# One fixed order for rows, weight halves and products at the three norm boundaries of a two-layer diffusion step, and a last norm shared by two engines

## The chip, the cores and the metric

The kernel runs on one core of one Trainium2 chip. The metric is the device time of one execution in microseconds (us), lower is better. The times before are those of three runs; besides these there is one profiled execution, from which every row below is taken.

The engines: PE multiplies matrices (PEld loads its weights), DVE and POOL work on vectors, ACT does activations and copies, SP issues the DMAs. Each engine works through its own queue in the order that stands in the built program.

## The reference, cut to what matters

Two groups of 128 tokens (a context pass and a denoising step, D_MODEL = 2048) go through two layers. Layer 0 mixes with MLA and GQA attention (`mixer_ab`), layer 1 with differential attention (`mixer_c`). Each mixer is followed by a gated convolutional feed-forward network (FFN). Ahead of each of these four sub-layers stands the same step:

```python
mod = jax.nn.silu(cond) @ w_ada[l] + b_ada[l]
sh1, sc1, gt1, sh2, sc2, gt2 = jnp.split(mod[:, None, :], 6, axis=-1)
h = rmsnorm(x, g_norm_mix[l]) * (1 + sc1) + sh1     # then the mixer
x = x + gt1 * m
h = rmsnorm(x, g_norm_ffn[l]) * (1 + sc2) + sh2     # then the FFN
x = x + gt2 * conv_ffn(h, ...)
...
return rmsnorm(x, g_final), ab_ctx, c_ctx
```

So no product of a sub-layer can start before the last residual of the one before it has gone into the norm's sum of squares. These places are called boundaries below. The change concerns three of them, between `mixer_ab` and FFN 0 (first), FFN 0 and `mixer_c` (second), `mixer_c` and FFN 1 (third), and the last norm at the end.

## The kernel before, in words

**Layout.** x lies in SBUF as 16 rows of blocks: `x[:, c]`, c = 0..15, is 128 features by 256 columns (128 tokens of each group). Every product is exact to float32 by splitting both sides in a high and a low part: three matmuls of 128x128 by 256 columns per block (wh times xh, wh times xl, wl times xh; lines 291 to 293 and 305 to 309). A chunk of output (128 features) needs 16 blocks of weights, so 48 matmuls, or 66 in the down projection.

**Weights.** A 1 MB tile `raw` (3 buffers) is loaded by SP and split in two halves of 8 blocks: ACT casts `wh` (line 212), DVE subtracts `wl` (line 213). `wh` and `wl` have 4 buffers each; one is free again when PE has used its 8 blocks. The four halves that `first_three` asks for at once (line 281) thus fill all four.

**A boundary, `modulated` (line 511).** PE sums the squares (`stat_rstd`, lines 192 and 193), POOL takes the power (179), DVE makes a diagonal (199), PE spreads it over all partitions (207). Then `modulate` (481) makes the 16 rows of the next input. A row is: DVE multiplies x by the norm's factor into `nt` (line 494, from PSUM), DVE scales and shifts the first group (500), ACT the second (503), ACT casts the high part into `hx` (504), DVE (every fourth row) or POOL subtracts the low part (489). `first_three` (275) runs the products of the first three chunks side by side, as the rows come. In the order AS_MADE chunk 1 follows two rows behind chunk 0, and chunk 2 two behind chunk 1; the last product thus comes four rows after the last row's first.

**Who sets the order.** Instructions are recorded in program order and then placed by a scheduler, which may move them on their engine's queue, unless `keep_in_program_order` pins them. Before, the rows and products of the second and third boundary are pinned (`fixed=True`), the weight halves there are not, and at the first boundary nothing is.

**Side work.** The `mod` vectors need 192 tiles of 1 MB of `w_ada`. They are computed in units: row units (`row_step`, line 406: four 1 MB tiles, each a group of matmuls at line 401, `sum_rows`, then a copy and four transposes) and feature units on DVE (line 386). `pump` spends them between chunks at the rates of `RATE` and `FRATE`; `RATE["heads"]` is that of the head loop of `mixer_ab`. `modulated` first calls `ensure` for the units that it needs, and computes one more row unit itself, with its tiles between the norm's steps (its third in the middle of the products).

**The FFN's first chunks.** `conv` (line 969) reads a chunk's sums out of PSUM (`pacc`, 3 buffers): ACT 974, DVE 977 and 980. At FFN 1 the first three are pinned and followed by the next weight half (`W.ahead`, line 233); at FFN 0 they aren't (`l > 0`).

**The end.** After the last norm (`norm_scale`) DVE makes the 16 products of x, g_final and the factor (line 1057), and SP writes four rows at a time (line 1060).

Of the kernel before, what the change touches and what calls it, by code (L numbers as in the profile page):

```python
# [47 lines left out]
    _AT[_name] = (_n, _w)  # L48
    _n += _w
NCONST = _n  # L50
RATE = {"in": 0.4, "in3": 0.25, "heads": 0.85, "out0": 1.2, "c": 0.65, "outc": 0.65}
FRATE = {"up": 0.7, "down": 1.42}
PEW = {"heads": 1.0, "out0": 1.0, "c": 0.5}
QUIET = [4, 3, 3]
LATE = 3
FINE = 4


LAG = 2
AS_MADE = [(c, i - LAG * c) for i in range(KD + 2 * LAG) for c in (2, 1, 0) if 0 <= i - LAG * c < KD]  # L60
IN_TURN = ([(c, k) for k in range(12) for c in range(3)] + [(c, k) for c in range(3) for k in range(12, KD)])
# [22 lines left out]
def step_kernel(ctx: ExitStack, tc: tile.TileContext, A: dict):  # L84
# [187 lines left out]
            out, self.blocks = self.blocks[:self.nblk], self.blocks[self.nblk:]  # L272
            return out

    def first_three(W, xh, xl, order, mid=None, fixed=False):


        pin = tc.keep_in_program_order if fixed else lambda i: i
        raws = [W.load() for _ in range(3)]
        ps = [T_(pacc, [P, 512], "acc") for _ in range(3)]  # L280
        blocks = {(c, h): W.halves(raws[c], 8 * h) for c, h in ((0, 0), (1, 0), (2, 0), (0, 1))}
        count = [0] * 3
        for n, (c, k) in enumerate(order):
            if mid and n == len(order) // 2:
                mid()
            if (c, k // 8) not in blocks:
                blocks[c, k // 8] = W.halves(raws[c], 8)
            wh, wl = blocks[c, k // 8][k % 8]
            a, b = count[c] == 0, count[c] == KD - 1
            count[c] += 1  # L290
            pin(pe.matmul(ps[c][:, :NT], wh, xh(k), start=a, stop=False))  # L291
            pin(pe.matmul(ps[c][:, :NT], wh, xl(k), start=False, stop=False))  # L292
            pin(pe.matmul(ps[c][:, :NT], wl, xh(k), start=False, stop=b))  # L293
        return [p[:, :NT] for p in ps]

    def gemm(blocks, xh, xl, n=NT, first=0, between=None):

# [183 lines left out]
    def modulate(hx, rb, l, which, chunks, fixed=False):  # L481


        pin = tc.keep_in_program_order if fixed else lambda i: i
        lows = []

        def low(c, h):
            eng = dve if (c % 4 == 0 if fixed else c % 2 == 0) else pool
            pin(eng.tensor_tensor(out=hx[:, c, NT:2 * NT], in0=h, in1=hx[:, c, :NT].bitcast(F32),
                                  op=ALU.subtract))  # L490

        for c in chunks:
            h = T_(tmp, [P, NT], "nt", bufs=4)
            pin(dve.tensor_tensor(out=h, in0=x[:, c], in1=rb, op=ALU.mult))
            for g in range(2):
                s = slice(g * T, (g + 1) * T)
                a_ = scl[:, l, which, c, g:g + 1]
                b_ = mod[:, l, 3 * which, c, g:g + 1]
                if g == 0:
                    pin(dve.tensor_scalar(out=h[:, s], in0=h[:, s], scalar1=a_, scalar2=b_,  # L500
                                          op0=ALU.mult, op1=ALU.add))
                else:
                    pin(act.activation(h[:, s], h[:, s], AF.Identity, scale=a_, bias=b_))
            pin(act.copy(hx[:, c, :NT], h))  # L504
            lows.append((c, h))
            if not fixed or len(lows) > 1:
                low(*lows.pop(0))
        for c, h in lows:
            low(c, h)

    def modulated(st, l, which, W, fixed):


        ensure(l, 3 * which + 1)
        ensure(l, 3 * which)
        while later:
            later.pop(0)()
        u = ROWS[ada["i"]]
        tile_ = lambda t: T_(wpool, [P, 4, 512], "araw", bufs=2)

        def load_tile(t):
            raw = tile_(t)
            sp.dma_start(out=raw, in_=A["w_ada"][u[0], u[1], u[2], t])
            return raw

        raws = [load_tile(0), load_tile(1)]
        hx = T_(keep, [P, KD, ROW], "hx", F32R)
        r = stat_rstd(st, D, att_bank)
        sum_rows(0, raws[0], bank())
        rb = spread(diagonal(r, (0, 1)), bank=att_bank)  # L530
        sum_rows(1, raws[1])
        raws += [load_tile(2), load_tile(3)]
        modulate(hx, rb, l, which, range(KD), fixed)
        ada["i"] += 1
        rest = ada_finish(*u, False)

        def last_rows():
            sum_rows(3, raws[3])
            rest[0]()

        def turn():
            rest[1](tc.keep_in_program_order)

        ps = first_three(W, lambda k: hx[:, k, :NT], lambda k: hx[:, k, NT:2 * NT],
                         AS_MADE if fixed else IN_TURN, lambda: sum_rows(2, raws[2]), fixed)
        if fixed:
            W.ahead(lambda i: i)
        return hx, ps, [last_rows, turn]

    def residual(ps, l, which, c, st=None):  # L550
        for g in range(2):
# [70 lines left out]
    def mixer_ab(hx, rb0, st):  # L622
        l = 0
        with tc.tile_pool(name="ab", bufs=1) as ab:
            with tc.tile_pool(name="abp", bufs=1) as pj:
# [107 lines left out]
                for q in range(4):  # L733
                    ensure(0, 1, [q])
                    ensure(0, 0, [q])
                    ada["both"] = False
                    pinned[0] = q == 3
                    if q == 3:
                        caches()
                    modulate(hx, rb0, 0, 0, range(4 * q, 4 * q + 4))  # L740
                    for c in range(23):
                        ps = gemm(W.chunk(), lambda k: hx[:, 4 * q + k, :NT], lambda k: hx[:, 4 * q + k, NT:2 * NT])
                        to = pr[:, c] if c < 15 else qb[:, c - 15]
                        if q == 0:
                            act.copy(to, ps)
                        else:
                            dve.tensor_tensor(out=to, in0=to, in1=ps, op=ALU.add)
                        if q == 3:
                            finish(c)
                        if q < 3:  # L750
                            pump(RATE["in"], until=2 * (q + 2))
                        else:
                            pump(RATE["in3"])

# [84 lines left out]
    def mixer_c(cp, hx, W, ready, todo, st):  # L839
# [108 lines left out]
        ready = first_three(W, oh, ol, LAST_LATE)  # L948
# [10 lines left out]
    def ffn(hx, W, ready, todo, l, st):  # L959
# [4 lines left out]
        with tc.tile_pool(name=f"ffn{l}", bufs=1) as fp, banks(f"pffn{l}") as pf:  # L964
# [2 lines left out]
            T_(fp, [P, SHIFT // 4], "pad")  # L967

            def conv(m):
                early = l > 0 and bool(ready)  # L970
                pin = tc.keep_in_program_order if early else lambda i: i
                ps = product()
                y = T_(fp, [P, NT], "cv", bufs=3)
                pin(act.activation(y, ps, AF.Identity, scale=cw[:, 1, m:m + 1], bias=cw[:, 3, m:m + 1]))  # L974
# [30 lines left out]
            def down(gs, q):  # L1005
                for c in range(KD):
                    quiet = q == NQ - 1 and c >= KD - QUIET[0]
                    fine[0] = quiet
                    ps = gemm(WD.chunk(), lambda k: gs[k][:, :NT], lambda k: gs[k][:, NT:2 * NT])
                    residual(ps, l, 1, c, st if q == NQ - 1 else None)  # L1010
                    pump(0, 0 if quiet else FRATE["down"])

            for q in range(NQ):
# [8 lines left out]
    with banks("pab") as ppool["ada"]:  # L1022
# [10 lines left out]
        st = stat_init()  # L1033
        mixer_ab(hx, rb0, st)
        W = Weights(A["w_up"][0], KD, 1)
        hx, ready, todo = modulated(st, 0, 1, W, False)
    stage[0] = "ffn0"
    st = stat_init()
    ffn(hx, W, ready, todo, 0, st)
# [1 line left out]
    with tc.tile_pool(name="cc", bufs=1) as cp, banks("pc") as ppool["ada"]:  # L1041
        ada["pool"] = cp
        ppool["att"] = ppool["ada"]
        W = Weights(A["w_in_c"], KD, 1)
        hx, ready, todo = modulated(st, 1, 0, W, True)
# [5 lines left out]
        hx, ready, todo = modulated(st, 1, 1, W, True)  # L1051
    stage[0] = "ffn1"
    st = stat_init()
    ffn(hx, W, ready, todo, 1, st)
    rb = norm_scale(st)
    for c in range(KD):
        dve.scalar_tensor_tensor(out=x[:, c], in0=x[:, c], scalar=C("gfin")[:, c:c + 1], in1=rb,  # L1057
                                 op0=ALU.mult, op1=ALU.mult)
        if c % 4 == 3:
            sp.dma_start(out=A["o_y"][:, c - 3:c + 1], in_=x[:, c - 3:c + 1])  # L1060

# [124 lines left out]
```

## Time and profile before

| what | us |
|---|---|
| median of three runs | 2388.5 (2387.7 to 2389.89) |
| the profiled execution | 2393.79 |
| its span, first to last instruction | 2391.9 |
| PE busy | 2329.2 |
| DVE busy | 1764.9 |
| ACT busy | 1165.7 |
| POOL busy | 180.2 |

A page of the profile gives the busy time of each engine, the chain that ended last and the costliest groups of instructions. Its views can be narrowed to a stretch of time: a timeline of one engine, groups by line, waits, and sums of several stretches (with PEclk, the clock granted to PE as a share of full speed). Times in a timeline count from the span's start; behind a row stands in brackets how long its engine was idle before it and what ended that.

### The profile page before, as it was taken

Reading aid. Unit: us, or ns where it says so; the run is one execution under the profiler, and the core shown is the slowest. Engines: PE = TensorE matmul, PEld = TensorE weight load, DVE = VectorE, ACT = ScalarE, POOL = GpSimd, SP = SyncE. Lnnn points to the kernel's source line nnn. Section 1 sums busy time; section 2 is a strip of 40 time slices with the busy share of each in tenths; the row PEclk is TensorE's granted clock in tenths of the full one; section 3 lists DMA queues with packets and bytes.
Section 4 is the critical chain, followed back from the end, with each engine's and each line's share of the span. In section 5 each row is a group of like instructions: output and inputs, shape, how many; then the busy total and the mean of one; then the engine's idle time right before and its main releaser. Section 6 shows DMA issues by size and latency. Waiting matters only on the chain. (4 is left out here: it accounts for less than half of the span.)

```text
span 2391.9 us, 47275 instructions
## 1 busy us (share of the span) xinstructions
PE 2329.2 (97%) x19664; PEld 2189.5 (92%) x19664; DVE 1764.9 (74%) x2691; ACT 1165.7 (49%) x1815; POOL 180.2 (8%) x219
## 2 busy tenths in 40 slices
PE   6999999999999999999999999999999999999997
PEld 3778868789999999999989999997999999999997
DVE  2467534469999999999979777877899855666654
ACT  4335544365554345554465444445655534555542
POOL 2002101110000000001220000023000000000011
PEclk9999999999999999999999999999999999999998
DMA  9886678877777777777766787686667655555553
GB/s 382 310 338 239 235 265 306 311 274 256 263 262 282 289 276 263 264 264 264 303 229 237 279 296 293 257 301 260 249 250 261 214 194 194 194 194 194 194 194 120
DMA packets 92549, 612.92 MB, mean 256 GB/s; under 512 B 9968, under 2 KB 17840, under 8 KB 20400
## 3 DMA queue, kind: packets, MB, share of 16 engines
q1 hardware_dynamic: 92336, 609.91, 69.6%
q8 instruction: 154, 2.52, 0.4%
q14 instruction: 59, 0.48, 0.1%
HBM read 605.12 MB, written 4.75 MB: 255 GB/s over the span
## 5 line engine op out<-in xcount | busy, mean ns | idle before, releaser
L212 ACT CAST wh<-raw 128x1024 fp32r<-128x1024 f32 (+1 forms) x788 | 795.5, 1015 | 984.0 <-PE acc L306 823.6
L213 DVE TENSOR_TENSOR wl<-raw,wh 128x1024 fp32r<-128x1024 f32 (+1 forms) x788 | 921.6, 1183 | 390.7 <-ACT wh L212 384.7
L305 PE MATMUL acc<-hx,wh 128*128 128x256 f32 x4064 | 1132.9, 279 | 8.6 <-ACT hx L504 5.6
L309 PE MATMUL acc<-hx,wl 128*128 128x256 f32 x4064 | 1131.0, 279 | 0.0
L306 PE MATMUL acc<-hx,wh 128*128 128x256 f32 x4064 | 1130.2, 278 | 0.0
L305 PEld LDWEIGHTS acc<-hx,wh 128*128 128x128 f32 x4064 | 765.9, 189 | 34.8 <-issue 12.1
L306 PEld LDWEIGHTS acc<-hx,wh 128*128 128x128 f32 x4064 | 766.5, 189 | 13.8 <-issue 12.9
L309 PEld LDWEIGHTS acc<-hx,wl 128*128 128x128 f32 x4064 | 766.2, 189 | 12.2 <-issue 10.4
L306 PE MATMUL acc<-g,wh 128*128 128x256 f32 x1408 | 388.3, 276 | 0.0
L309 PE MATMUL acc<-g,wl 128*128 128x256 f32 x1408 | 388.0, 276 | 0.0
L305 PE MATMUL acc<-g,wh 128*128 128x256 f32 x1408 | 387.8, 276 | 0.0
L386 DVE CUSTOM_DVE_ANT_0 junk<-araw,condb 128x2048 f32<-128x2048 f32 x120 | 275.0, 2291 | 0.0
L306 PEld LDWEIGHTS acc<-g,wh 128*128 128x128 f32 x1408 | 264.3, 188 | 0.0
L309 PEld LDWEIGHTS acc<-g,wl 128*128 128x128 f32 x1408 | 264.2, 188 | 0.0
L305 PEld LDWEIGHTS acc<-g,wh 128*128 128x128 f32 x1408 | 264.1, 188 | 0.0
L172 POOL TENSOR_TENSOR sqacc<-sqacc,sq 128x256 f32<-128x256 f32 x76 | 93.0, 1223 | 1534.1 <-issue 1223.1
L401 PE MATMUL ada<-araw,condw 128*32 128x512 f32 x768 | 106.6, 628 | 19.3 <-DMA araw<-w_ada 18.5
L430 DVE SCALAR_TENSOR_TENSOR aacc<-araw,condw,aacc 128x512 f32<-128x512 f32 x150 | 111.8, 773 | 0.2
L553 DVE SCALAR_TENSOR_TENSOR x<-acc,mod,x 128x128 f32<-128x128 f32 x192 | 58.3, 345 | 56.5 <-PE acc L309 55.5
L974 ACT ACTIVATE cv<-acc,convw 128x256 f32<-128x256 f32 x176 | 98.5, 560 | 1.4 <-PE acc L293 1.4
L980 DVE SCALAR_TENSOR_TENSOR cv<-acc,convw,cv 128x254 f32<-128x254 f32 x176 | 84.4, 480 | 3.5
L977 DVE SCALAR_TENSOR_TENSOR cv<-acc,convw,cv 128x254 f32<-128x254 f32 x176 | 83.8, 476 | 2.6 <-ACT cv L974 2.5
(221 smaller groups left out, 1840.1 us busy)
## 6 DMA issues: line engine op xcount, KB each, us to landing
araw<-w_ada SPq DMA_DIRECT2D x188, 1024.0 KB, 5.8
raw<-w_up SPq DMA_DIRECT2D x176, 1024.0 KB, 4.8
raw<-w_down SPq DMA_DIRECT2D x88, 1024.0 KB, 4.8
raw<-w_in_c SPq DMA_DIRECT2D x48, 1024.0 KB, 5.0
raw<-w_in_ab SPq DMA_DIRECT2D x20, 1024.0 KB, 7.0
raw<-w_out_ab SPq DMA_DIRECT2D x16, 1024.0 KB, 6.8
raw<-w_out_c SPq DMA_DIRECT2D x16, 1024.0 KB, 5.2
raw<-w_q_up SPq DMA_DIRECT2D x6, 768.0 KB, 4.7
```

The costliest lines, as they stand in the source:

```text
L172: pool.tensor_tensor(out=st["acc"], in0=st["acc"], in1=sq, op=ALU.add)
L212: pin(act.copy(out_hi, src))
L213: pin(dve.tensor_tensor(out=out_lo, in0=src, in1=out_hi.bitcast(F32), op=ALU.subtract))
L305: fixed(pe.matmul(ps[:, :n], wh, xh(k), start=(i == 0), stop=False))
L306: fixed(pe.matmul(ps[:, :n], wh, xl(k), start=False, stop=False))
L309: fixed(pe.matmul(ps[:, :n], wl, xh(k), start=False, stop=(i == last)))
L386: tc.keep_in_program_order(dve.tensor_tensor_reduce(out=T_(feat["pool"], [P, D], "junk"), in1=feat["row"][:, c], in0=feat["raw"].rearrange ...
L401: i = pe.matmul(ada["ps"][32 * g:32 * g + 32, :], condw[:, 4 * t + g, :], raw[:, g], start=(t == 0), stop=(t == 3), skip_group_check=True)
L430: i = dve.scalar_tensor_tensor(out=acc[:, c], in0=raw[:, g], scalar=condw[:, k, c:c + 1], in1=acc[:, c], op0=ALU.mult, op1=ALU.add)
L974: pin(act.activation(y, ps, AF.Identity, scale=cw[:, 1, m:m + 1], bias=cw[:, 3, m:m + 1]))
L977: pin(dve.scalar_tensor_tensor(out=y3[:, :, 1:], in0=p3[:, :, :T - 1], scalar=cw[:, 0, m:m + 1], in1=y3[:, :, 1:], op0=ALU.mult, op1=ALU.add))
L980: pin(dve.scalar_tensor_tensor(out=y3[:, :, :T - 1], in0=p3[:, :, 1:], scalar=cw[:, 2, m:m + 1], in1=y3[:, :, :T - 1], op0=ALU.mult, op1=A ...
```

## The change

1. `modulate` becomes a generator that yields after each row (and once more at the end). It runs pinned at all three boundaries.
2. `first_three` becomes a class `Three`: `prepare(c, h)` makes half h of chunk c's weights, now pinned as well; `add(c, k)` the three products of one block.
3. `modulated` interleaves them in one order for all three boundaries. Two rows come first, then half (0, 0), and then per step of AS_MADE: one more row, what PREP asks for, and the step's products. `W.ahead` (pinned too) is called behind it.
4. At FFN 0 the first three chunks are pinned, as at FFN 1.
5. `RATE["heads"]` goes from 0.85 to 1.05, so that row units are done earlier; the first boundary then has none of them left but its own.
6. The last norm: for five of the 16 rows ACT multiplies by g_final right after the row's last residual, and POOL multiplies by a copy of the factor in SBUF (made by ACT); DVE does the other eleven. The output goes in five pieces of 4, 4, 4, 2 and 2 rows.

```diff
-RATE = {"in": 0.4, "in3": 0.25, "heads": 0.85, "out0": 1.2, "c": 0.65, "outc": 0.65}
+RATE = {"in": 0.4, "in3": 0.25, "heads": 1.05, "out0": 1.2, "c": 0.65, "outc": 0.65}
+EARLY = (2, 5, 8, 11, 13)
+SENT = (4, 8, 12, 14, 16)
-AS_MADE = [(c, i - LAG * c) for i in range(KD + 2 * LAG) for c in (2, 1, 0) if 0 <= i - LAG * c < KD]
+AS_MADE = [[(c, i - LAG * c) for c in (2, 1, 0) if 0 <= i - LAG * c < KD] for i in range(KD + 2 * LAG)]
+PREP = {0: (1, 0), 2: (2, 0), 5: (0, 1), 8: (1, 1), 10: (2, 1)}
+AHEAD = 2
...
+        def prepare(self, c, h):
+            if (c, h) not in self.blocks:
+                self.blocks[c, h] = self.W.halves(self.raws[c], 8 * h, self.pin)
...
-        modulate(hx, rb, l, which, range(KD), fixed)
...
-        ps = first_three(W, lambda k: hx[:, k, :NT], lambda k: hx[:, k, NT:2 * NT],
-                         AS_MADE if fixed else IN_TURN, lambda: sum_rows(2, raws[2]), fixed)
-        if fixed:
-            W.ahead(lambda i: i)
-        return hx, ps, [last_rows, turn]
+        rows = modulate(hx, rb, l, which, range(KD), True)
+        for _ in range(AHEAD):
+            next(rows)
+        three.prepare(0, 0)
+        for i, steps in enumerate(AS_MADE):
+            next(rows, None)
+            if i in PREP:
+                three.prepare(*PREP[i])
+            if i == len(AS_MADE) // 2:
+                sum_rows(2, raws[2])
+            for c, k in steps:
+                three.add(c, k, lambda k: hx[:, k, :NT], lambda k: hx[:, k, NT:2 * NT])
+        W.ahead(lambda i: i)
+        return hx, three.sums(), [last_rows, turn]
...
-                early = l > 0 and bool(ready)
+                early = bool(ready)
...
+                    if l == NL - 1 and q == NQ - 1 and c in EARLY:
+                        act.activation(x[:, c], x[:, c], AF.Identity, scale=C("gfin")[:, c:c + 1])
...
+    rbs = T_(tmp, [P, NT], "nt", bufs=4)
+    act.copy(rbs, rb)
+    sent = 0
     for c in range(KD):
-        dve.scalar_tensor_tensor(out=x[:, c], in0=x[:, c], scalar=C("gfin")[:, c:c + 1], in1=rb,
-                                 op0=ALU.mult, op1=ALU.mult)
-        if c % 4 == 3:
-            sp.dma_start(out=A["o_y"][:, c - 3:c + 1], in_=x[:, c - 3:c + 1])
+        if c in EARLY:
+            pool.tensor_tensor(out=x[:, c], in0=x[:, c], in1=rbs, op=ALU.mult)
+        else:
+            dve.scalar_tensor_tensor(out=x[:, c], in0=x[:, c], scalar=C("gfin")[:, c:c + 1], in1=rb,
+                                     op0=ALU.mult, op1=ALU.mult)
+        if c + 1 in SENT:
+            sp.dma_start(out=A["o_y"][:, sent:c + 1], in_=x[:, sent:c + 1])
+            sent = c + 1
```

In the built program the queues of ACT and DVE at a boundary stand thus, the same at all three (r0 is row 0; wh00 is the cast of half 0 of chunk 0; wlA that of `W.ahead`; a row's parts are named by their lines):

```
before, second and third boundary
  ACT: wh00 wh10 wh20 wh01 (among the last residuals' squares), then r0: 503 504, r1: 503 504, ... r10;
       the other three casts among the rows 10 to 14
  DVE: wl00 wl10 wl20 wl01 (likewise), then r0: 494 500, r1: 494 500, 489, r2: 494 500, ...
after, all three boundaries
  ACT: r0: 503 504, r1: 503 504, wh00, r2, wh10, r3, r4, wh20, r5, r6, r7, wh01, r8, r9, r10, wh11,
       r11, r12, wh21, whA, r13, r14, r15
  DVE: r0: 494 500, r1: 494 500, 489, wl00, r2: 494 500, wl10, r3, r4, wl20, r5, r6, r7, wl01, r8, r9,
       r10, wl11, r11, r12, wl21, r13: 494, wlA, 500, r14, r15 (489 for every fourth row among them)
```

Before the change DVE's queue at the third boundary has one wl of the next sub-layer directly ahead of the last residual (line 553) and one behind it. In the changed program the last residual has none of them ahead of it. The order of PE's queue at the second and third boundary is the same before and after. The number of matmuls, weight casts and loads of weights is the same in both programs.

More of the change, by code (lines that the diff above doesn't have):

```diff
@@ L273, in chunk, with __init__, add, sums @@
             return out
[L275 to L294, printed above, removed]
+    class Three:
+        def __init__(self, W, pin):
+            self.W, self.pin = W, pin
+            self.raws = [W.load() for _ in range(3)]
+            self.ps = [T_(pacc, [P, 512], "acc") for _ in range(3)]
+            self.count = [0] * 3
+            self.blocks = {}
+        def prepare(self, c, h):
+            if (c, h) not in self.blocks:
+                self.blocks[c, h] = self.W.halves(self.raws[c], 8 * h, self.pin)
+        def add(self, c, k, xh, xl):
+            self.prepare(c, k // 8)
+            wh, wl = self.blocks[c, k // 8][k % 8]
+            a, b = self.count[c] == 0, self.count[c] == KD - 1
+            self.count[c] += 1
+            ps = self.ps[c][:, :NT]
+            self.pin(pe.matmul(ps, wh, xh(k), start=a, stop=False))
+            self.pin(pe.matmul(ps, wh, xl(k), start=False, stop=False))
+            self.pin(pe.matmul(ps, wl, xh(k), start=False, stop=b))
+        def sums(self):
+            return [p[:, :NT] for p in self.ps]
     def gemm(blocks, xh, xl, n=NT, first=0, between=None):
@@ L507, in modulate, with modulated @@
                 low(*lows.pop(0))
+            yield
         for c, h in lows:
             low(c, h)
-    def modulated(st, l, which, W, fixed):
+        yield
+    def modulated(st, l, which, W):
         ensure(l, 3 * which + 1)
@@ L527, in modulated @@
         hx = T_(keep, [P, KD, ROW], "hx", F32R)
+        three = Three(W, tc.keep_in_program_order)
         r = stat_rstd(st, D, att_bank)
@@ L739, in mixer_ab @@
                         caches()
-                    modulate(hx, rb0, 0, 0, range(4 * q, 4 * q + 4))
+                    for _ in modulate(hx, rb0, 0, 0, range(4 * q, 4 * q + 4)):
+                        pass
                     for c in range(23):
@@ L947, in mixer_c @@
         oh, ol = (lambda k: o_all[:, k, :NT]), (lambda k: o_all[:, k, NT:2 * NT])
-        ready = first_three(W, oh, ol, LAST_LATE)
+        three = Three(W, lambda i: i)
+        for c, k in LAST_LATE:
+            three.add(c, k, oh, ol)
+        ready = three.sums()
         for c in range(KD):
@@ L1035, in step_kernel @@
         W = Weights(A["w_up"][0], KD, 1)
-        hx, ready, todo = modulated(st, 0, 1, W, False)
+        hx, ready, todo = modulated(st, 0, 1, W)
     stage[0] = "ffn0"
@@ L1044, in step_kernel @@
         W = Weights(A["w_in_c"], KD, 1)
-        hx, ready, todo = modulated(st, 1, 0, W, True)
+        hx, ready, todo = modulated(st, 1, 0, W)
         load_cw(1)
@@ L1050, in step_kernel @@
         W = Weights(A["w_up"][1], KD, 1)
-        hx, ready, todo = modulated(st, 1, 1, W, True)
+        hx, ready, todo = modulated(st, 1, 1, W)
     stage[0] = "ffn1"
```

1 line of the change is left out of this document (removed).

## The prediction

> **What bounds the kernel now.** The page first: PE is busy nearly throughout, so only what makes PE wait counts.
>
> ```profile
> span 2391.9 us, 47275 instructions
> PE 2329.2 (97%) x19664; PEld 2189.5 (92%) x19664; DVE 1764.9 (74%) x2691; ACT 1165.7 (49%) x1815; POOL 180.2 (8%) x219
> ```
>
> Then sums of stretches: a long one inside FFN 0, the three boundaries and the end (columns: stretch, length, busy time of PE, PEld, DVE, ACT, POOL with counts, PEclk).
>
> ```profile
> 472.60:502.80 30.20, 27.74 (x216) 19.59 (x214) 21.18 (x52) 18.32 (x41) 7.13 (x9) 1.00 0.79 306
> 502.80:509.00 6.20, 3.75 (x19) 3.78 (x20) 5.33 (x10) 4.51 (x7) 0.00 (x0) 0.72 0.97 396
> 512.00:1210.00 698.00, 698.00 (x6161) 698.00 (x6160) 634.18 (x795) 347.58 (x453) 24.85 (x14) 1.00 0.73 266
> 1210.30:1238.20 27.90, 23.77 (x183) 19.21 (x181) 22.41 (x47) 19.43 (x40) 11.39 (x13) 1.00 0.66 246
> 1641.90:1673.40 31.50, 26.38 (x179) 20.07 (x179) 23.80 (x49) 20.43 (x42) 11.30 (x13) 0.89 0.69 267
> 2376.80:2391.90 15.10, 2.14 (x11) 1.28 (x9) 7.61 (x21) 0.42 (x1) 0.70 (x1) 0.57 0.34 139
> ```
>
> In FFN 0 PE does 6161 matmuls in 698.00 us, 0.113 us each, without a pause. At a boundary it does about 180 in 28 to 31 us, where 180 x 0.113 = 20.4 would do. So a boundary's length is set not by PE but by what feeds it. PE's and DVE's timelines mark the parts: last matmul of the old sub-layer, first row (494), last product (293).
>
> ```profile
> 472.45 0.28 PE L309 MATMUL acc<-hx,wl 128*128 128x256 f32 x1
> 502.49 0.28 PE L293 MATMUL acc<-hx,wl 128*128 128x256 f32 x1
> 505.25 0.55 PE L305 MATMUL acc<-hx,wh 128*128 128x256 f32 x1 [2.49 <-ACT cv L974]
> 1210.18 0.28 PE L309 MATMUL acc<-g,wl 128*128 128x256 f32 x1
> 1237.94 0.28 PE L293 MATMUL acc<-hx,wl 128*128 128x256 f32 x1
> 1641.56 0.28 PE L309 MATMUL acc<-oall,wl 128*128 128x256 f32 x1
> 1673.09 0.28 PE L293 MATMUL acc<-hx,wl 128*128 128x256 f32 x1
> ```
>
> ```profile
> 477.19 1.42 DVE L494 TENSOR_TENSOR nt<-x,att 128x256 f32<-128x256 f32 x4 [0.79 <-PE att L207]
> 1214.97 0.42 DVE L494 TENSOR_TENSOR nt<-x,att 128x256 f32<-128x256 f32 x1 [0.79 <-PE att L207]
> ```
>
> The norm (last matmul to first row) takes 4.74 us at the first boundary and 4.79 at the second. The rows and products (first row to last product) take 25.30 and 22.97. The third boundary, in more detail:
>
> ```profile
> 1642.99 1.23 DVE L213 TENSOR_TENSOR wl<-raw,wh 128x1024 fp32r<-128x1024 f32 x1 [4.53 <-ACT wh L212]
> 1644.14 0.60 DVE L553 SCALAR_TENSOR_TENSOR x<-acc,mod,x 128x128 f32<-128x128 f32 x2
> 1649.80 0.42 DVE L494 TENSOR_TENSOR nt<-x,att 128x256 f32<-128x256 f32 x1 [1.55 <-PE att L207]
> 1650.26 0.34 DVE L500 TENSOR_SCALAR nt<-nt,scl,mod 128x128 f32<-128x128 f32 x1
> 1650.52 0.41 DVE L494 TENSOR_TENSOR nt<-x,att 128x256 f32<-128x256 f32 x1
> 1652.02 0.91 DVE L500 TENSOR_SCALAR nt<-nt,scl,mod 128x128 f32<-128x128 f32 x1
> ```
>
> ```profile
> 1641.92 1.99 ACT L212 CAST wh<-raw 128x1024 fp32r<-128x1024 f32 x2 [4.39 <-PE acc L309]
> 1650.26 0.50 ACT L503 ACTIVATE nt<-nt,mod,scl 128x128 f32<-128x128 f32 x1 [5.00 <-DVE nt L494]
> 1650.79 0.41 ACT L504 CAST hx<-nt 128x256 fp32r<-128x256 f32 x1
> 1651.10 0.49 ACT L503 ACTIVATE nt<-nt,mod,scl 128x128 f32<-128x128 f32 x1
> ```
>
> Here the norm takes 1649.80 - 1641.56 = 8.24 us: the last residual (553) stands behind a wl that waits for its cast. Rows and products take 23.29.
>
> **The change part by part.** *The norm.* At the third boundary nothing stands ahead of the last residual any more, so I give it the 4.8 of the other two: -3.4. At those two it stays.
>
> *The rows.* Before, ACT and DVE have made four halves when the rows begin, in the norm's waits. The change puts all of them behind row 1, in a fixed order on both queues. That order closes a ring: wl follows the cast on another engine; the next row's first step (494) stands behind wl on DVE; that row's ACT steps need it; the next cast stands behind those. So halves and rows no longer overlap. The price of one turn (a cast, its wl, a row), by the rows above and this view of the groups of 1642 to 1674 (count, busy, mean ns):
>
> ```profile
> L489 POOL TENSOR_TENSOR hx<-nt,hx 128x256 fp32r<-128x256 f32 x12 | 10.6, 882 | 12.4 <-ACT hx L504 12.2
> L500 DVE TENSOR_SCALAR nt<-nt,scl,mod 128x128 f32<-128x128 f32 x16 | 7.9, 492 | 0.5
> L213 DVE TENSOR_TENSOR wl<-raw,wh 128x1024 fp32r<-128x1024 f32 x6 | 7.5, 1258 | 4.8 <-ACT wh L212 4.8
> L212 ACT CAST wh<-raw 128x1024 fp32r<-128x1024 f32 x7 | 7.2, 1043 | 4.4 <-PE acc L309 4.4
> ```
>
> - the cast 1.04, and 0.03 until wl starts (1641.92 + 1.04 = 1642.96; wl at 1642.99)
> - wl until DVE's next: 1644.14 - 1642.99 = 1.15
> - 494 until the ACT step 503: 0.46 (1649.80 to 1650.26)
> - 503 until 504: 0.53; 504 until ACT's next: 0.31 (1650.26, 1650.79, 1651.10)
>
> Sum 3.52 us a turn. There are six turns (halves 00, 10, 20, 01, 11, 21, each followed by a row). Ahead of the first stand rows 0 and 1: 0.46 + 2 x 0.84 = 2.14. Eight rows follow a row directly (r4, 6, 7, 9, 10, 12, 14, 15), at ACT's 0.84: 6.72. The half of `W.ahead` stands between row 13's 494 and 500, so its cast part is not cheaper but wl lies in the row's way: 0.33 + 1.15 + 0.38 in place of 0.99, +0.87. And POOL's subtraction blocks a 500 now and then: the one at 1652.02 took 0.91 instead of 0.34, while POOL ran:
>
> ```profile
> 1652.10 0.74 POOL L489 TENSOR_TENSOR hx<-nt,hx 128x256 fp32r<-128x256 f32 x1 [4.37 <-ACT hx L504]
> ```
>
> In turns the subtraction lies beside the cast, so it can hit only the eight direct rows. Bounds: 0, and 8 x 0.57 = 4.6; I take two at 0.7, 1.4, near the share before (16 x (0.49 - 0.34) = 2.4 us for 16 rows). Sum: 2.14 + 21.12 + 6.72 + 0.87 + 1.4 = 32.25. Behind it come row 15's subtraction with the waits around it (0.9) and the 20 matmuls that are left by the lag of the chunks (20 x 0.113 = 2.3): 35.5 us from first row to last product, where the 144 products need 16.3 of PE. The two rows of lead that the order gives PE are used up after two turns.
>
> Second boundary: 35.5 - 22.97 = +12.5. Third: 35.5 - 23.29 - 3.4 = +8.8. First: 35.5 - 25.30 = +10.2.
>
> *FFN 0's first chunks pinned.* PE's 2.49 us of waiting at 505.25 for ACT's reading of the sums goes, and so does the half clock behind it (PEclk 0.72 in 6.2 us, 1.7 us): 2.6 + 1.7 = -4.3. What is late next: casts at their own pace, as at the third boundary, where PE went on at once after 1673.09.
>
> *Heads' rate.* The same units, earlier. Four groups of a row unit leave the first boundary:
>
> ```profile
> L401 PE MATMUL ada<-araw,condw 128*32 128x512 f32 x32 | 4.3, 605 | 1.6 <-DMA araw<-w_ada 1.6
> ```
>
> Their 4.3 us now fall into the head loop and the output projection, where PE has hardly a pause: +4.3. Bounds: 0 (if they fill waits for the softmax there) and 4.3; I take 4.3, since the long gaps are few. Their loads are the same and go ahead earlier on SP. First boundary in all: 10.2 - 4.3 + 4.3 = +10.2.
>
> *The end.*
>
> ```profile
> 2381.71 6.36 DVE L1057 SCALAR_TENSOR_TENSOR x<-x,cst,misc 128x256 f32<-128x256 f32 x16 [1.38 <-PE misc L207]
> 2383.40 5.03 SPq L1060 DMA_DIRECT2D o_y<-x  x4
> 11.89 11.18 POOL L172 TENSOR_TENSOR sqacc<-sqacc,sq 128x256 f32<-128x256 f32 x14 [10.65 <-ACT sq L168]
> ```
>
> DVE does 16 in 6.36, 0.39 each; eleven take 4.4. POOL does one in 0.80 (11.18 / 14); five take 4.0, behind ACT's copy (about 0.5, as 504). Both end at about 2386.2 instead of 2388.1, and the piece with POOL's last row goes out one issue (0.34) ahead of the last: -1.5. Bounds: -1.9, and +1.7 if the two engines exclude each other (11 x 0.39 + 5 x 0.74 = 8.0). The 494s above read x and PSUM as line 1057 does and were not lengthened by POOL, so I take -1.5. The five ACT products lie beside a chunk of 66 matmuls, 7.5 us: nothing.
>
> Sum: 12.5 + 8.8 + 10.2 - 1.5 = **+30.0**. The profiled execution would take 2393.8 + 30 = 2423.8; it stood 5.3 over the median, so the median goes from 2388.5 to **2418.5**.
>
> *A rule against it.* The clock fell to half behind 2.49 us without a matmul, the pause that ended at 505.25. The rule of the Trainium skill, "TensorE: Matmul & The Clock Gate", "Part 1: The HAM clock gate", says that PE goes to half clock after an idle window of about 3.4 us; by it the pauses of a turn would cost nothing. The trace differs: less than that was enough.
>
> **The rivals.** *Half clock in the ring.* The longest pause I expect is one turn less its matmuls, about 1.7 us, but in the first turns PE has only three to six matmuls in 3.5 us, less than a third. If that counts as idle, much of the stretch runs at 0.21 us a matmul; ACT and DVE hide that, except for the last 20 matmuls: +2.3 each time, and some more in the later turns, about +3 each: 2427.
>
> *Heads wait for loads.*
>
> ```profile
> 205.00:376.00 171.00, 164.43 (x1173) 128.71 (x1172) 86.77 (x242) 83.64 (x200) 18.05 (x50) 1.00 0.69 250
> ```
>
> With 1.05 / 0.85, so 23%, more units there (most of the head loop is the stretch above, where PE stands still for 6.57 of 171 us), a group may wait for its tile. The group above waited 1.6 us; at that price for the five or six groups more: +9, 2428. Against it: the DMA share is 0.69 there, less than in the 0.79 and 0.97 about the first boundary.
>
> *Partial ring.* Moved groups covered, no POOL conflict, all turns 0.2 shorter: -4.3 - 4.2 - 3.6, 2406.
>
> *Faster.* If the halves overlap with the rows after all (ACT or DVE passing a waiting instruction), rows and products stay at about 23 and the gains stand alone: -3.4 - 4.3 - 1.5, 2379. The point: the ring must cost less than 3.1 us a boundary. Against it: at 1644.14 DVE did hold a ready residual (PE was done at 1641.84) behind a wl whose cast was late. That the order isn't kept falls with it: it stands in the built program.
>
> **How the numbers follow.** Forecast 0.72 (2409 to 2425 by its bounds), half clock 0.08, heads 0.05, partial ring 0.07, faster 0.06; no visible change 0.02. A measurement can tell about 0.2% (4.8 us) from no change. Faster 0.06, same 0.02, slower 0.92. The range takes in partial ring and both slower rivals: 2404 to 2430.
>
> **What would show it.** In the changed profile: first row to last product near 35 us at all three boundaries, alike; DVE's 213 there waiting for ACT's 212 and ACT's 503 for DVE's 494 seven times each; PE idle for ACT and DVE about 15 us each time; the third norm 4.8 us; no pause at FFN 0's fourth chunk; line 1088's POOL products at 0.8. Wrong would be: 494 starting while a cast that stands ahead of its wl is still running.

## The result, and the profile after

The changed kernel takes 2425.0 us (median of 4 runs, 2422.7 to 2427.9) against 2389.2 us before (4 runs): a ratio of 1.0147, 95% interval 1.0132 to 1.0163. Forecast were 2418.5 us, 2404 to 2430, and slower with a chance of 0.92. The profiled execution took 2426.1 us, with a span of 2424.3; against the one of before that is +32.3, where the working had +30.0.

From the changed kernel's page: PE's busy time grew by 19 us although it does the same 19664 matmuls, and its clock drops at the boundaries.

```profile
span 2424.3 us, 47258 instructions
PE 2347.8 (97%) x19664; PEld 2201.3 (91%) x19664; DVE 1758.8 (73%) x2682; ACT 1166.9 (48%) x1821; POOL 176.7 (7%) x228
PEclk8999999989999999999989999998999999999999
```

PE's timeline of the changed kernel, the last matmul of each old sub-layer (319) and the last product behind each norm (301); then DVE's, the first row of each (504, which was 494 before).

```profile
472.56 0.28 PE L319 MATMUL acc<-hx,wl 128*128 128x256 f32 x1
...
515.37 0.28 PE L301 MATMUL acc<-hx,wl 128*128 128x256 f32 x1
...
1218.80 0.28 PE L319 MATMUL acc<-g,wl 128*128 128x256 f32 x1
...
1260.92 0.28 PE L301 MATMUL acc<-hx,wl 128*128 128x256 f32 x1
...
1663.48 0.28 PE L319 MATMUL acc<-oall,wl 128*128 128x256 f32 x1
...
1706.70 0.28 PE L301 MATMUL acc<-hx,wl 128*128 128x256 f32 x1
...
2410.13 0.28 PE L319 MATMUL acc<-g,wl 128*128 128x256 f32 x1
```

```profile
477.69 0.42 DVE L504 TENSOR_TENSOR nt<-x,att 128x256 f32<-128x256 f32 x1 [1.31 <-PE att L211]
...
1223.61 0.42 DVE L504 TENSOR_TENSOR nt<-x,att 128x256 f32<-128x256 f32 x1 [0.99 <-PE att L211]
...
1668.61 0.42 DVE L504 TENSOR_TENSOR nt<-x,att 128x256 f32<-128x256 f32 x1 [1.31 <-PE att L211]
```

Subtracting these from each other gives the whole account. "Rest" is what a stretch, from one old sub-layer's last matmul to the next one's, changed by beside its norm and its rows and products. Each row is rounded by itself.

| part | before | after | change | forecast |
|---|---|---|---|---|
| start to the first boundary | 472.45 | 472.56 | +0.1 | +4.3 |
| first boundary: norm | 4.74 | 5.13 | +0.4 | 0 |
| rows and products | 25.30 | 37.68 | +12.4 | +10.2 |
| rest, FFN 0 | | | -4.3 | -4.3 |
| second boundary: norm | 4.79 | 4.81 | 0.0 | 0 |
| rows and products | 22.97 | 37.31 | +14.3 | +12.5 |
| rest, `mixer_c` | | | -1.1 | 0 |
| third boundary: norm | 8.24 | 5.13 | -3.1 | -3.4 |
| rows and products | 23.29 | 38.09 | +14.8 | +12.2 |
| rest, FFN 1 | | | 0.0 | 0 |
| end (last old matmul to the span's end) | 15.4 | 14.2 | -1.2 | -1.5 |
| sum | | | +32.4 | +30.0 |

All three boundaries are now alike at 37 to 38 us. The ring is in the rows. First DVE's timeline of the second boundary, then ACT's:

```profile
1226.80 1.23 DVE L217 TENSOR_TENSOR wl<-raw,wh 128x1024 fp32r<-128x1024 f32 x1 [1.35 <-ACT wh L216]
1227.94 0.42 DVE L504 TENSOR_TENSOR nt<-x,att 128x256 f32<-128x256 f32 x1
1228.39 0.35 DVE L510 TENSOR_SCALAR nt<-nt,scl,mod 128x128 f32<-128x128 f32 x1
1230.30 1.23 DVE L217 TENSOR_TENSOR wl<-raw,wh 128x1024 fp32r<-128x1024 f32 x1 [1.56 <-ACT wh L216]
```

```profile
1225.73 1.04 ACT L216 CAST wh<-raw 128x1024 fp32r<-128x1024 f32 x1
1228.39 0.49 ACT L513 ACTIVATE nt<-nt,mod,scl 128x128 f32<-128x128 f32 x1 [1.62 <-DVE nt L504]
1228.92 0.41 ACT L514 CAST hx<-nt 128x256 fp32r<-128x256 f32 x1
1229.23 1.04 ACT L216 CAST wh<-raw 128x1024 fp32r<-128x1024 f32 x1
```

Read them across: ACT casts from 1225.73, DVE waits 1.35 us for that and subtracts, then makes the row's 504; ACT has waited 1.62 us for that 504, and casts again at 1229.23. A turn is 1229.23 - 1225.73 = 3.50 us, in which each engine stands still for the other. 3.52 was forecast.

The windows of the changed kernel show what I had put among the rivals (columns as before; the last but two is PEclk): the long stretch in the head loop, then the second boundary: the last 3.41 us ahead of its rows, the ring's first turns, and its last stretch, whole and in two parts.

```profile
205.00:376.00 171.00, 167.43 (x1193) 127.44 (x1192) 86.20 (x243) 83.25 (x200) 16.56 (x50) 1.00 0.75 275
...
1219.63:1223.04 3.41, 2.19 (x16) 1.20 (x16) 0.81 (x5) 0.42 (x1) 0.70 (x1) 1.00 0.52 154
1223.60:1233.60 10.00, 6.67 (x24) 3.81 (x24) 6.26 (x13) 5.94 (x12) 1.98 (x3) 0.50 0.55 203
...
1253.60:1261.20 7.60, 7.25 (x50) 7.25 (x50) 3.12 (x6) 4.22 (x8) 2.22 (x3) 0.78 0.36 140
1253.80:1257.10 3.30, 3.15 (x14) 3.15 (x15) 1.80 (x5) 1.96 (x5) 2.21 (x3) 0.50 0.75 295
1257.20:1261.00 3.80, 3.80 (x34) 3.80 (x34) 0.92 (x1) 1.91 (x3) 0.00 (x0) 1.00 0.05 15
```

In the ring's first turns PE does 24 matmuls in 10 us and has half its clock all the time. PE waits for a cast in each of these turns anyway, so I count no cost there. In the last stretch it has 0.78: half clock until 1257.1, while the last rows come, and full clock when PE alone is left to finish.

### The profile page after: what moved, and what is told of

Its sections match the earlier page's. It is cut to its first block, busy times and chain, and to the rows that moved or that the text cites. A ratio compares the mean times of both kernels' runs of the same rounds, so it can differ in the third digit from the quotient of the medians.

```text
span 2424.3 us, 47258 instructions
## 1 busy us (share of the span) xinstructions
PE 2347.8 (97%) x19664; PEld 2201.3 (91%) x19664; DVE 1758.8 (73%) x2682; ACT 1166.9 (48%) x1821; POOL 176.7 (7%) x228
## 4 chain that ended last, share of the span: by engine, by line
PE 91%; DMA 3%; DVE 3%; ACT 2%; issue 2%; POOL 0%; SPq 0%; DVEq 0%; ACTq 0%; POOLq 0%
PE acc L315 27%; PE acc L316 27%; PE acc L319 27%; PE ada L411 4%; DMA araw<-w_ada 1%; DVE wl L217 1%; PE att L623 1%; ACT wh L216 1%; PE acc L300 1%; DMA ckc<-cache_ckv 1%; PE acc L299 1%; PE acc L301 1%; DVE nt L510 0%; DMA raw<-w_in_ab 0%; ACT nt L513 0%
## 5 line engine op out<-in xcount | busy, mean ns | idle before, releaser
L315 PEld LDWEIGHTS acc<-hx,wh 128*128 128x128 f32 x4064 | 764.3, 188 | 29.3 <-issue 12.5
L1002 DVE SCALAR_TENSOR_TENSOR cv<-acc,convw,cv 128x254 f32<-128x254 f32 x176 | 83.5, 475 | 10.3 <-ACT cv L999 10.2
```

Source lines behind the costliest of these rows:

```text
L315: fixed(pe.matmul(ps[:, :n], wh, xh(k), start=(i == 0), stop=False))
```

## The experiments

Of each run the time is given as a ratio to the kernel before, run on the same chip (95% interval). There the kernel before took 2390.8 to 2391.6 us, about 2 us more than in the first comparison, from which the expected times start. In the table, columns 3 to 7 come from each run's trace, in the manner of the account above: last old matmul to first row (norm), and first row to last product (rows) at the three boundaries.

| run | ratio | heads* | rows 1 | rows 2 | rows 3 | third norm |
|---|---|---|---|---|---|---|
| before | 1 | 278.4 | 25.3 | 23.0 | 23.3 | 8.2 |
| after | 1.0147 | 279.4 | 37.7 | 37.3 | 38.1 | 5.1 |
| e1 | 0.9993 | 278.6 | 25.9 | 25.3 | 25.1 | 5.6 |
| e2 | 1.0036 | 279.5 | 29.0 | 29.4 | 29.4 | 5.2 |
| e3 | 1.0038 | 278.7 | 27.0 | 28.2 | 27.9 | 7.0 |
| e4 | 0.9952 | 278.6 | 20.9 | 23.0 | 22.9 | 5.3 |
| e5 | 1.0380 | 279.0 | 55.8 | 55.6 | 58.1 | 5.1 |
| e6 | 0.9962 | 279.0 | 23.0 | 23.3 | 22.9 | 4.8 |
| e7 | 0.9949 | 278.7 | 20.9 | 22.8 | 20.9 | 5.6 |
| e8 | 0.9985 | 278.0 | 25.3 | 23.6 | 22.9 | 8.0 |
| e9 | 1.0120 | 278.8 | 35.4 | 36.2 | 35.9 | 5.1 |
| e10 | 1.0245 | 277.7 | 44.0 | 38.3 | 38.3 | 5.1 |

*from the program's second norm, inside `mixer_ab` (at 194.1 us before), to the last old matmul of the first boundary. What lies ahead of that norm was edited in none of these runs, but its length differs between the profiled executions (190.8 us in e8, 196.9 in e2), so it is left out.

**e1: the pin off the halves alone.**

```diff
-                self.blocks[c, h] = self.W.halves(self.raws[c], 8 * h, self.pin)
+                self.blocks[c, h] = self.W.halves(self.raws[c], 8 * h)
```

Expected:

> The changed kernel with only the pin on the weight halves taken off; rows and products stay pinned and recorded in the same places. Theory (the fixed order of halves and rows is a serial ring): the first halves go back into the norm's waits, first row to last product falls from 37.3-37.7 us to 23-25.5 us at each boundary, and the time from 2425.0 to 2384-2391, since the stall of FFN 0 (4.3) and the end (1.2) stay gained; a third norm of over 5 us would put it at the upper end. Rival (the interleaving of rows and products on PE, or the half clock, is what costs): it stays above 2410.

Measured: 2389.2 us, 0.9993 (0.9983 to 1.0002). One pin removed takes away the loss. DVE's timeline of this run shows where the halves went:

```profile
1205.07 1.23 DVE L217 TENSOR_TENSOR wl<-raw,wh 128x1024 fp32r<-128x1024 f32 x1 [1.49 <-ACT wh L216]
...
1207.80 1.23 DVE L217 TENSOR_TENSOR wl<-raw,wh 128x1024 fp32r<-128x1024 f32 x1 [0.34 <-ACT wh L216]
...
1212.06 0.42 DVE L504 TENSOR_TENSOR nt<-x,att 128x256 f32<-128x256 f32 x1 [1.56 <-PE att L211]
```

Both, and two more (at 1199.82 and 1202.35), stand ahead of the first row: three beside the last matmuls of the old sub-layer, which end at 1206.46, and one in the norm's waits. The interleaving as such was kept here, so it isn't what costs; but it gains nothing either: rows 2 and 3 take 25 us, before they took 23, and the whole gives back what the other edits gain (e4).

**e2: all pinned, but each wl one row later.**

```diff
...
-        three.prepare(0, 0)
+        lows = []
+        three.prepare(0, 0, lows)
         for i, steps in enumerate(AS_MADE):
             next(rows, None)
+            while lows:
+                lows.pop(0)()
             if i in PREP:
-                three.prepare(*PREP[i])
+                three.prepare(*PREP[i], lows)
...
```

(`prepare` makes the cast at once and puts the subtraction into `lows`.)

Expected:

> The changed kernel with everything pinned as it is, but each half's subtraction (wl) put behind the next row instead of ahead of it. Theory of the ring: in the 2.68 us from a cast's start to the next 503 (cast 1.04 + 0.03, wl 1.15, 494 0.46) one more row is done, so each of six turns gives 0.84 us: 5.0 a boundary, 15 in all, 2410 (2406-2414); the distance from one cast to the next in neighbouring turns falls from 3.50 us to about 1.9-2.7. Rival (the engines' work in that stretch is the bound, not its order): 2425, no change. Rival (PE at half clock is the bound): first row to last product falls by less than 2 us a boundary, 2419 or more.

Measured: 2400.7 us, 1.0036 (1.0022 to 1.0049); 24 us less than the changed kernel, more than the 11 to 19 expected. The casts of the second boundary on ACT's timeline:

```profile
1221.18 1.04 ACT L216 CAST wh<-raw 128x1024 fp32r<-128x1024 f32 x1
1222.96 1.04 ACT L216 CAST wh<-raw 128x1024 fp32r<-128x1024 f32 x1
1226.52 1.04 ACT L216 CAST wh<-raw 128x1024 fp32r<-128x1024 f32 x1
```

The first two casts, with one row between them, stand 1.78 us apart instead of 3.50; the next two, with two rows between them, 3.56 instead of 4.52 (1229.23 to 1233.75 in the changed kernel). The engines and their work are the same, and so is the order on ACT; each wl was moved by one row on DVE. So the ring is the order, not the work. From the first cast to the sixth the run needs 18.1 us (1221.18 to 1239.27) where the changed kernel needs 23.8 (1225.73 to 1249.54), 5.7 less, as expected (5.0). The other 2 us here lie behind the sixth cast, where PE now has full clock (PEclk 1.00 from 1239.27 to 1248.49).

**e3: all pinned, four halves ahead of the norm.**

```diff
         three = Three(W, tc.keep_in_program_order)
+        for c, h in ((0, 0), (1, 0), (2, 0), (0, 1)):
+            three.prepare(c, h)
```

Expected:

> The changed kernel, all pinned, but the four halves 00, 10, 20, 01 are recorded ahead of the norm instead of between the rows; 11 and 21 stay in their places. Theory of the ring: two turns are left of six; rows and products 25-28 us, the norm longer by about 2 (three wl stand between the diagonal and the first row, 3 x 1.15 less the 1.1-1.6 us that DVE waits there): each boundary 9 to 12 us shorter, 2389-2398. If pinning alone cost the time, it stays above 2415.

Measured: 2401.7 us, 1.0038 (1.0025 to 1.0051), 4 us over the upper end of what was expected. The rows came to 27 to 28 us, as the upper end had it. The norm became 3 us longer at the first two boundaries (8.1 us each) instead of 2, and 1.8 at the third. This run's DVE, behind the diagonal:

```profile
1213.77 3.49 DVE L217 TENSOR_TENSOR wl<-raw,wh 128x1024 fp32r<-128x1024 f32 x3
1217.17 0.41 DVE L504 TENSOR_TENSOR nt<-x,att 128x256 f32<-128x256 f32 x1
```

Three wl stand ahead of the first row and delay it. Pinned early, the halves cost in the norm part of what they save later; left loose (e1) three of the four lie ahead of the norm.

**e4: the kernel before with the three other edits.**

```diff
-RATE = {"in": 0.4, "in3": 0.25, "heads": 0.85, "out0": 1.2, "c": 0.65, "outc": 0.65}
+RATE = {"in": 0.4, "in3": 0.25, "heads": 1.05, "out0": 1.2, "c": 0.65, "outc": 0.65}
...
-                early = l > 0 and bool(ready)
+                early = bool(ready)
...
+        if c in EARLY:
+            pool.tensor_tensor(out=x[:, c], in0=x[:, c], in1=rbs, op=ALU.mult)
...
```

Expected:

> The kernel before with the three other edits alone: units' rate 1.05 in the heads, FFN 0's first chunks pinned, the end on two engines; order of rows, halves and products untouched. From the changed kernel's trace: the stall of FFN 0 gone (-4.3), the end -1.2, the rate 0: 2389.2 - 5.5 = 2383.7 (2382-2386). If the moved row units cost what I forecast (+4.3 ahead of the first boundary): 2388. If FFN 0's pinned chunks only gain with the fixed order: 2388 too, but then with the pause still at the fourth chunk.

Measured: 2380.6 us, 0.9952 (0.9935 to 0.9968): 10.8 us less than before, twice what was expected. Two gains came on top. First row to last product at the first boundary fell from 25.30 to 496.28 - 475.33 = 20.95, and the third norm from 8.24 to 5.3, though neither place was edited. FFN 0 gave 3.4 us in this order (last product to last matmul: 707.7 before, 704.3 here), the end its 1.2. DVE's and PE's rows of this run:

```profile
475.33 1.41 DVE L496 TENSOR_TENSOR nt<-x,att 128x256 f32<-128x256 f32 x4 [1.31 <-PE att L209]
```

```profile
496.28 0.28 PE L295 MATMUL acc<-hx,wl 128*128 128x256 f32 x1
```

**e8: the same, with the heads' rate back at 0.85.**

```diff
-RATE = {"in": 0.4, "in3": 0.25, "heads": 1.05, "out0": 1.2, "c": 0.65, "outc": 0.65}
+RATE = {"in": 0.4, "in3": 0.25, "heads": 0.85, "out0": 1.2, "c": 0.65, "outc": 0.65}
```

Expected:

> The run e4 with the heads' rate back at 0.85. Theory (the four moved groups lie in pauses of the head loop, and free the first boundary where no ring covers them): first row to last product at the first boundary 25.3 instead of 20.9, the head loop and output projection 0.2-1.0 shorter: 2380.6 + 3.4 to 4.2 = 2384-2385. By my forecast the groups cost 4.3 in the heads: the stretch before the first boundary 4.3 shorter, 2380-2381.

Measured: 2386.9 us, 0.9985 (0.9976 to 0.9993), 6.3 us above e4. The heads became 0.5 us shorter, not 4.3, and the first boundary's rows are back at 25.3: theory held, my forecast's 4.3 fell. The third norm is back at 8.0 too. A load explains that. The DMA view of the third weight tile of the third boundary, in the kernel before:

```profile
L229 SPq DMA_DIRECT2D raw<-w_up x1: 328/328/328, 1633.8 to 1633.8; - x1
...
DMA to landing us min/median/max: 8.0/8.0/8.0
```

It lands at 1633.8 + 8.0 = 1641.8, and the cast for which that wl and the last residual waited starts at 1641.92. The profile puts this wait down to PE, whose last old matmul ended at nearly the same time (1641.84). In e8 the tile lands at 1636.6, and there the profile names the load:

```profile
1636.70 1.99 ACT L214 CAST wh<-raw 128x1024 fp32r<-128x1024 f32 x2 [4.17 <-DMA raw<-w_up]
```

In e4 it lands at 1629.5, nearly 2 us ahead of the last matmul (1631.44). In all three runs at 0.85 (before, e8, e10) the tile is issued 7.8 us ahead of the last old matmul and lands behind it; in all the others it is issued 9.1 us ahead and lands at least 1.2 us ahead. In the kernel before and in e8 a load of `w_ada` was issued 2.9 us ahead of it, between it and the tile before; in e4 none stands there. How a rate in the head loop moves that order a thousand us later stays open.

**e10: the changed kernel with the rate back at 0.85.** The edit is that of e8.

Expected:

> The changed kernel with the heads' rate back at 0.85. Theory: under the ring the four groups are covered at the first boundary (first row to last product 37.7, at most 40), the stretch before it is 0.3-1.0 shorter, and the third weight tile of the third boundary lands late as in both runs at 0.85 so far, so that the third norm takes about 8 us instead of 5.1: 2425 + 2 = 2427 (2425-2430). Rival (the groups cost their 4.3 in the heads): the stretch before the first boundary 4.3 shorter, 2421. Rival (the late tile was chance): the third norm stays at 5.1, 2424-2425.

Measured: 2445.8 us, 1.0245 (1.0188 to 1.0301). The four runs lie apart, two at 2431 and 2433, two at 2458 and 2460; the profile is of the fastest, and what the other two lost isn't known. In the profile three expectations fell. The stretch before the boundary is 1.7 us shorter, more than the 0.3 to 1.0 expected. The groups are not covered: rows 1 take 44.0. ACT's timeline and PE's:

```profile
479.82 0.59 ACT L352 COPY am<-ada 128x512 f32<-128x512 f32 x1 [9.47 <-PE ada L411]
480.30 0.49 ACT L513 ACTIVATE nt<-nt,mod,scl 128x128 f32<-128x128 f32 x1
```

```profile
477.76 1.94 PE L411 MATMUL ada<-araw,condw 128*32 128x512 f32 x8 [1.65 <-DMA araw<-w_ada]
```

The unit's last group waits for its tile, the copy of the unit's sum waits for the group, and that copy stands ahead of the first row's 513 on ACT: it starts 6.8 us behind the row's 504 (at 473.52), where the changed kernel needs 0.5. So the ring starts 6.3 us late, and the rows are 6.3 us longer. And the third norm stayed at 5.1 although the third tile landed at 1668.2, as late as before (last old matmul 1667.97): in the changed order no half stands ahead of the last residual. So the change cures that wait by its order, and the rate cures it by the load; either is enough.

**e5 and e9: matmuls in PE's waits.**

```diff
             for c, k in steps:
                 three.add(c, k, lambda k: hx[:, k, :NT], lambda k: hx[:, k, NT:2 * NT])
+            for _ in range(FILL.get(i, 0)):
+                three.pin(pe.matmul(fill[:, :NT], three.blocks[0, i // 8][0][0], hx[:, 0, :NT], start=True, stop=True))
```

(e9, with FILL = {0: 16, 1: 8, 2: 12, 5: 12, 8: 12, 10: 10}; e5 had 86 of them, of two constants, ahead of the products.)

Expected of e5:

> The changed kernel with 86 extra matmuls a boundary (constants times constants into a PSUM bank that nobody reads), placed in PE's waits of the turns, so that the clock stays up. Theory (beside the ring, the half clock behind these waits costs the 2 us a boundary by which 37.3-38.1 us stand over my 35.5): the turn from cast to cast stays 3.50 us, first row to last product falls to 35.5-36 at each boundary, the time to 2419-2420. Rival (the excess is the lag of the chunks, not the clock): no change, 2425. Rival (PE, not the ring, is the bound): 86 x 0.113 = 9.7 more a boundary, 2454.

Measured: 2481.2 us, 1.0380 (1.0366 to 1.0394). That told nothing of the clock, since the matmuls were too dear. Its group of them at the second boundary:

```profile
L569 PE MATMUL att<-cst 128*128 128x256 f32 x171 | 38.1, 380 | 0.0
```

38.1 us for 86 (two records each), 0.44 a piece: PE became the bound.

Expected of e9:

> The run e5 mended: its extra matmuls took 0.45 us each, not 0.113, so PE became the bound. Here 70 extra matmuls a boundary use a ready weight half and row 0 (0.113 us each, 7.9 us), placed behind the products of the steps that wait for a turn, none in the last ten steps. Theory (half clock behind the turns' waits costs about 2 us a boundary): turn 3.50 us as before, first row to last product 35.5-36.2, 2419-2421. Rival (the excess over 35.5 is the lag of the chunks): 37.3-38.1 as in the changed kernel, 2425. Rival (PE's own work is the bound): 7.9 more a boundary, 2448.

Measured: 2421.8 us, 1.0120 (1.0105 to 1.0135). Windows of e9's second boundary, beside those of the changed kernel above:

```profile
1221.30:1231.30 10.00, 7.85 (x44) 5.91 (x45) 6.25 (x13) 5.94 (x12) 1.99 (x3) 0.73 0.50 197
...
1251.30:1257.60 6.30, 5.84 (x47) 5.64 (x48) 3.00 (x7) 4.05 (x8) 2.23 (x3) 1.00 0.50 204
```

70 matmuls more, and every boundary is 1.1 to 2.3 us shorter: PEclk is 1.00 instead of 0.78 in the end, and first row to last product is 35.4, 36.2 and 35.9, near the 35.5 of my sum. The turn stayed at 3.50 us (casts at 1223.43 and 1226.93). So of the 1.8 to 2.6 us by which the changed kernel stands over 35.5, the half clock explains 1.1 to 2.3.

**e6 and e7: e4 with its rows pinned at all boundaries, or at none.**

```diff
-        hx, ready, todo = modulated(st, 0, 1, W, False)
+        hx, ready, todo = modulated(st, 0, 1, W, True)
```

(e6; e7 has False at the second and third.)

Expected of e6:

> The run e4 with its first boundary's rows and products pinned too, in the order of the other two (halves loose). Theory (pinned rows cost little, pinned halves cost the time): first row to last product at the first boundary from 20.9 to the 22.9-23.0 of the other two, +2.0: 2382.6. Rival (pinning the rows there is part of the change's loss): over 26 us there, 2386 or more.

Measured: 2381.3 us, 0.9962 (0.9948 to 0.9975); rows 1 at 23.0, as expected. Pinning rows and products without the halves costs 2 us, not 12. The switch does two more things besides pinning: it takes the products in the order AS_MADE instead of IN_TURN, and it gives DVE every fourth of the low-part subtractions instead of every second one. The 2 us belong to all three together, and so does e7's gain.

Expected of e7:

> The run e4 with rows and products loose at the second and third boundary as well, in the order of the first (IN_TURN, no lag). Theory (the loose order is the shorter one, 20.9 against 23.0 and 22.9): -4.1, 2376.5. Rival (the first boundary is short for another reason, such as the tiles that lie ready there): no change, 2380.6, or slower.

Measured: 2378.2 us, 0.9949 (0.9936 to 0.9961). The third boundary came to 20.9 as expected, the second only to 22.8; why that one differs stays open. e4, e6 and e7 all beat both kernels, and their intervals overlap.

## Why the prediction was right, and where it failed

- **The ring** was right in mechanism and price: 3.50 us a turn against 3.52; the last row's subtraction ended 33.5 us behind the first row's start (1223.61 to 1255.53 + 1.58 = 1257.1, by the POOL row below) against 33.15. e1, e2 and e3 each break it in another way, and each time the rows and products fall by 8 to 13 us. DVE waits for ACT's cast six times at this boundary, not seven: the wl of `W.ahead` follows a cast that was done by then. That half is not pinned in either kernel, against item 3 of the change: its call passes `lambda i: i`, which pins nothing; its place among the last rows is the scheduler's.

```profile
1255.53 1.58 POOL L499 TENSOR_TENSOR hx<-nt,hx 128x256 fp32r<-128x256 f32 x2 [0.65 <-ACT hx L514]
```

- **The catch-up behind it** was mis-sized: "20 matmuls that are left by the lag" at 0.113, 2.3 us, took 3.8 at the second boundary (1257.1 to 1260.92). PE had full clock there, about 0.12 us a matmul, but 33 were left instead of 20: from 1253.8 to 1257.1, at half clock, it had done 14 in 3.3 us almost without a pause. PE stood still for 8.0 to 8.5 us at each boundary, not 15, with 29.2 to 29.8 us busy at a clock of 0.71 to 0.76. The rival of the half clock (+3 a boundary) was right beside the forecast, not in its place: +1.1 to +2.3 by e9. The rule of the Trainium skill that the prediction named ("TensorE: Matmul & The Clock Gate", "Part 1: The HAM clock gate") differs from these traces too: it asks for an idle window of about 3.4 us, and at the second boundary PEclk was 0.50 though no two neighbouring matmuls started more than 2.45 us apart.
- **The heads' rate** is the term that failed: "where PE has hardly a pause: +4.3". The forecast took PE's 6.57 us of standing still in 205 to 376 as too little; they became 3.57, with 20 matmul records more in that stretch. The heads' stretch took 278.6 to 279.5 us in the nine runs at 1.05 and 277.7 to 278.4 in the three at 0.85, so the groups cost about 1 us there, not 4.3; the lower of my two bounds was the better value. That the account has only +0.1 comes from the 0.9 us by which the part ahead of the heads was shorter in this execution. What the groups cost at the place that they left wasn't priced at all: 6.3 us by e10 (44.0 against 37.7), 4.3 by e8 against e4. The rival of heads that wait for loads (+9) did not come.
- **FFN 0's stall**: -4.3, as forecast, as the rest of that stretch. **The POOL conflict**: three 510s of the second boundary took 0.78, 0.91 and 0.69 instead of 0.34, 1.4 us in all, as forecast.
- **The third norm**: -3.1 against -3.4. The wl ahead of the residual was the right place, but its cast stood behind a late load, which the rows quoted there didn't show.
- **The end**: -1.2 against -1.5. DVE and POOL did not hinder each other, as forecast, but DVE now starts behind ACT's copy of the factor, 5.39 us after the last old matmul instead of 5.19:

```profile
2415.52 4.40 DVE L1090 SCALAR_TENSOR_TENSOR x<-x,cst,misc 128x256 f32<-128x256 f32 x11 [1.58 <-ACT nt L1084]
```

```profile
2415.57 3.46 POOL L1088 TENSOR_TENSOR x<-x,nt 128x256 f32<-128x256 f32 x5 [2.15 <-ACT nt L1084]
```

Eleven of DVE's take 4.40, 0.40 each, and five of POOL's 3.46, 0.69 each, side by side (forecast: 4.4 and 4.0).

So 4.2 too much for the heads, 6.6 too little for three boundaries' rows, 1.0 too little for the norms and the end, and 1.1 less in `mixer_c` that stays unexplained leave the sum 2.4 short. That it is so near is partly luck: the error at the heads hid most of the one at the rows. The other 4 us between 2418.5 and 2425.0 are an assumption on the profiles: I let the changed kernel's profiled execution stand 5.3 us over its median, as that of before did, and it stood 1.1 over.

## What to carry to other kernels

Before two streams of work are put into one fixed order, follow the order across the engines: where A's second step stands ahead of B's first on one engine, and B's second ahead of A's first on the other, each turn costs the sum of both, however idle the engines are. Moving one step by one item (e2), or leaving one of the streams to the scheduler (e1), breaks that. And price moved work at both ends: at the place it goes to by the pauses there, and at the place it leaves by what waited behind it, its loads too.

## What the runs showed of the hardware

Half clock does not need a long idle: PE did 24 matmuls in the 10 us at PEclk 0.50, and 20 more in such a stretch brought it to 0.73 (e9). At the second boundary of the changed kernel it came ahead of the ring's first turn, at 1223.0, behind 3.41 us with 16 matmuls (some of one column only) that started at most 1.15 us apart; the ring then kept it until 1240.1. And a matmul of two plain float32 constants took 0.44 us, four times the 0.113 of the kernel's own of the same shape; it shows as two records.
